# Where the operand sets of a transformer layer's last MLP third are made, and where a second set of buffers starts in memory

## The chip, the cores and the metric

The kernel runs on one core of one Trainium2 chip. The metric is the device time of one execution in microseconds (us); the time before is the median of three runs, 1019.47 us (1018.25, 1019.47 and 1020.26). Engines are named as in the profile: PE (TensorE), PEld (TensorE's weight load), DVE (VectorE), ACT (ScalarE), POOL (GpSimd), SP (SyncE, whose queue issues nearly all transfers).

## The reference

One decoder layer over 256 tokens of width 2048, in float32. Cut to what matters here:

```python
h = rms_norm(x, attn_norm_g)
proj = h @ w_in                       # q, k, v of 8 heads, and a pooled part
x = x + concat([attention(q, k, v), pooled(p)]) @ w_out

h = rms_norm(x, ffn_norm_g)           # the gated MLP; D_FF = 5632
u = h @ w_up                          # 2048 -> 2 * 5632
y = conv_b + sum(conv_w[i] * shifted(u, i) for i in range(3))
gate, val = split(y, 2)
x = x + (silu(gate) * val) @ w_down   # 5632 -> 2048
```

All matrix products keep float32 accuracy: each operand is split into a rounded high part and a low remainder, and three products (high by high, low by high, high by low) are summed.

## The kernel before

**Steps.** The whole kernel is a list of 362 steps. Each step uses one tile of weights of 128 x 1024 numbers. Two such tiles form a chunk of 1 MB, which SP loads into one of four `raw` buffers, in the order of use (`in_order`, line 131). Before a step, ACT makes the high part `wh` (`split_high`, line 163) and DVE the low part `wl` (`split_low`, line 167), five to six steps ahead of PE. DVE and ACT work strictly in the order in which the program emits their instructions, so what is emitted in a step's hooks (`after(u, f)`, line 622) stands in one line with the splits for the steps that follow. A chunk's `raw` buffer is released when its second tile has been split, and the release issues the next load (`release`, line 227).

**Stages.** Steps 0 to 97 hold the attention and the mixer, with a last block of 16 steps, the mixer's output projection by pairs. From step 98 the MLP runs in three thirds (`THIRDS`, line 57) of 8, 8 and 6 groups of 256 hidden columns. A third has an up projection of 8 steps for each group (64, 64, 48 steps), in which each group's gate and value pass through the convolution on DVE and ACT (`conv`, line 718: `L524` reads the value out of the PE's accumulators, then `L728`, `L735`, and later `L754`, `L761`), and then a down projection in two passes `b` = 0, 1 over output halves of 1024 columns, with one "quad" `j` of two steps for each group (16, 16, 12 steps a pass). In the text, "first third, up 14" is the step 14 after the first third's start. An up step and an ordinary half quad take 12 to 16 matmuls.

**Sums in place of products.** Some quads (`MIXED`, line 58) are done in the manner of Strassen and Winograd with 7 products in place of 8 (`quad_sums`, line 839: 12 matmuls of 512 columns in its first half, 9 in its second). Such a quad needs an operand set: sums and differences of the weights' quarters (`form_sums`, line 188), split in high and low, kept in a tile of 3072 numbers per partition. There are two such tiles. `s0` (index 0) belongs to a pool that lives through the whole MLP. `s1` (index 1) is opened anew for each down projection, behind a small tile `row`, in a pool whose memory the convolution's tiles `fs` and `y` use at other times (`open_temps`, line 634, with the down projection's opening at its step 2). Which quads use `s1` is set by `SECOND` (line 59) and `OUT_SECOND` (line 63): two of the mixer's, four in the first third, four in the second, two in the third, together 12. In the program before, `s0` starts 128 bytes past a multiple of 512 bytes in its partition, as all `wh` and `wl` buffers do when they are used in a down projection, and `s1` 64 bytes past one. In an operand set's quad, 9 of the 21 matmuls stream the set's columns through PE.

**Sets made early.** For most of these quads the set is made just before the quad. For two quads of each third it is made early, in the up projection, and parked in device memory (`STORED`, line 60). For such a quad, at an up step `at`:

- the chunk is loaded a first time as an extra chunk between two others (line 143), and for that time holds one of the four `raw` buffers;
- hook `at`: `early_sums` (line 193), on DVE one `L213` of 512 columns, one `L189` of 1024, one `L190` and one `L191` of 512, and one ACT copy;
- hook `at + 1`: `early_split` (line 198), one ACT copy and one `L213` of 1024 columns on DVE, and the release of the buffer;
- hook `at + 3`: `early_store` (line 202), two transfers from SP's queue to device memory, 0.5 MB of `t13` and 1.5 MB of `s0`, which serves as the scratch tile.

Later the quad's chunk is loaded in two halves, one of them from the stored `t13` (lines 136 and 137), and hook `u - ahead` loads the stored set of 1.5 MB (`load_set`, line 207, `L208`) into the quad's tile.

In the program before, each third makes its own two: the first and second third at up 22 and up 38, the third at up 22 and up 30. The third's two are for pass 0, quad 4 and pass 1, quad 2; both quads use `s1`. In the first quad of a down projection the second output accumulator takes over the bank that the last group's value was in, so its first matmul waits until `L524` of the last group has read that bank.

Of the kernel before, what the change touches and what calls it, by code (L numbers as in the profile page):

```python
# [25 lines left out]
F32 = mybir.dt.float32  # L26
# [5 lines left out]
P = 128  # L32
# [24 lines left out]
THIRDS = ((0, 8), (8, 16), (16, 22))  # L57
MIXED = {8: ((0, 3, 5, 6), (0, 3, 5, 6)), 6: ((0, 3, 4), (0, 2, 3))}
SECOND = {8: ((5,), (0, 3, 6)), 6: ((4,), (2,))}
STORED = {8: ((0, 5, 7), (1, 5, 6)), 6: ((0, 4, 5), (1, 2, 6))}  # L60
SUMMED = {n: sorted(set(a + b)) for n, (a, b) in MIXED.items()}
OUT_MIXED = (2, 3, 5, 6)
OUT_SECOND = (3, 6)
# [25 lines left out]
def layer(ctx: ExitStack, tc: tile.TileContext, xT, xtok, wts, par, rel_d, ident_d, icnt_d, out):  # L89
# [28 lines left out]
    raws, wparts, shift, late = {}, {}, {}, {}  # L118
    seven, stored, extra = {}, {}, {}
# [82 lines left out]
    def early_store(c):  # L202
        stored[c] = (dram.tile([P, HALF], F32, name=f"t{c}"), dram.tile([P, 3072], F32, name=f"s{c}"))
        nc.sync.dma_start(stored[c][0], late["t13"])
        nc.sync.dma_start(stored[c][1], late["tile"][0].bitcast(F32))

    def load_set(c, i):
        nc.sync.dma_start(late["tile"][i].bitcast(F32), stored[c][1])  # L208
# [370 lines left out]
    steps, hooks = [], []  # L579
# [29 lines left out]
    def feat_block(act, post, alloc=acc):  # L609
        box, runs = {}, []  # L610
        for i, k0 in enumerate(XK):
            def run(u, i=i, k0=k0):
                if i == 0:
                    box["ps"] = alloc("ps_feat")
                feat_half(u, act(), k0, box["ps"], i == 0, i == 3)
                if i == 3:
                    post(box["ps"])
            run.shift = SHIFT
            runs.append([run])
        return runs  # L620

    def after(u, f):

        hooks.append((u, f))

    def seven_tiles(pool, i):
        s = pool.tile([P, 3072], F32R, name=f"s{i}", tag=f"s{i}")
        late.setdefault("tile", {})[i] = s
        return [[s[:, :512], s[:, 512:1024]], [s[:, 1024:2048], s[:, 2048:]]]
# [4 lines left out]
    def open_temps(down):  # L634

        if "ctx" in late:
            late["ctx"].close()
        late["ctx"] = ExitStack()
        late["temps"] = late["ctx"].enter_context(tc.tile_pool(name="temps", bufs=1))
        if down:  # L640
            late["temps"].tile([P, 72], F32, name="row")
            late["s"][1] = seven_tiles(late["temps"], 1)

    def open_heads():
# [5 lines left out]
    def open_late():  # L650
        ectx.close()
        pool = ctx.enter_context(tc.tile_pool(name="late", bufs=1))
        late["pool"] = pool
        late["x2"] = pool.tile([P, NT, D], F32, name="x2")
        nc.sync.dma_start(late["x2"], xtok)
        sx = pool.tile([P, 4, 4, 2, P], F32R, name="sx")
        late["sx"] = [sx[:, i] for i in range(4)]
        late["s"] = [seven_tiles(pool, 0), None]
        open_temps(False)
        late["ss"] = pool.tile([P, NT, D // 512], F32, name="ss")  # L660
        late["t13"] = pool.tile([P, HALF], F32, name="t13")
# [80 lines left out]
    def gate(ps, g):  # L742
        def then(y):
            nc.scalar.activation(y, y, AF.Silu)
            late["gate"] = y
        conv(ps, 2 * g, 0, then)

    def value(ps, g, j):
        if j == 0:
            late["hid"] = keep.tile([P, KT, 2, S], F32R, name="hid", tag="c")  # L750
        hid, ks, mixed = late["hid"], slice(2 * j, 2 * j + 2), j in late["mixed"]

        def then(y):
            nc.vector.tensor_tensor(y, y, late["gate"], op=OP.mult)  # L754
            nc.scalar.activation(hid[:, ks, 0, :], y, AF.Copy)  # L755
            if mixed:
                token_sums(y)
            late["y"] = y

        def low():  # L760
            nc.vector.tensor_tensor(hid[:, ks, 1, :], late["y"], hid[:, ks, 0, :].bitcast(F32), op=OP.subtract)  # L761
            if mixed:
                sums_split(j, part=0)

        conv(ps, NF + 2 * g, 1, then)
        later(3, low)
        if mixed:
            later(4, lambda: sums_split(j, part=1))
# [272 lines left out]
    for b in range(2):  # L1041
# [3 lines left out]
        at = st["q", b, "end"] + (3 if b else 7)  # L1045
        if b == 0:
            after(at - 6, lambda: st.__setitem__(("q", 0), head_norm(st["qraw"], "qn", keep, "c")))
        for j in range(4):
            h, u = 4 * b + j, at + 2 * j
# [17 lines left out]
    for i, j in enumerate(OUT_MIXED):  # L1067
        after(o0 + 6 + 2 * i, lambda j=j: mixed_sums(OUT_ORDER[j]))
        after(o0 + 7 + 2 * i, lambda i=i: sums_split(i))
    after(len(steps) - 1, lambda: open_temps(True))  # L1070
    steps += down_pair(1, 8, False, "mixer")
    f0 = len(steps)
    after(f0 - 1, lambda: open_temps(False))
    after(f0 - 1, lambda: x2_T(1))
    after(f0 - 1, lambda: [square_sum(b, t) for t in range(NT) for b in (2, 3)])
# [2 lines left out]
    after(f0 + 3, lambda: x2_T(3))  # L1078
    after(f0 + 4, row2)

    for n, (g0, g1) in enumerate(THIRDS):
        nq, u0 = g1 - g0, len(steps)
        for i, (b, j, ahead) in enumerate(STORED[nq]):
            u = u0 + 8 * nq + b * 2 * nq + 2 * j
            at = u0 + 22 + 2 * nq * i - 4 * i * (nq < 8)
            extra[(at + 4) // 2] = u // 2
            after(at, early_sums)
            after(at + 1, early_split)
            after(at + 3, lambda c=u // 2: early_store(c))
            after(u - ahead, lambda c=u // 2, i=int(j in SECOND[nq][b]): load_set(c, i))  # L1090
        after(len(steps), lambda nq=g1 - g0: late.__setitem__("mixed", range(len(SUMMED[nq]))))
        for g in range(g0, g1):
            one = feat_block(lambda: late["h"], lambda ps, g=g: gate(ps, g),
                             acc if g > g0 else smalls if n else aux)
            two = feat_block(lambda: late["h"], lambda ps, g=g, j=g - g0: value(ps, g, j))
            steps += one + two if g else [step for both in zip(one, two) for step in both]
        after(len(steps) + 2, lambda: open_temps(True))
        for bp in range(2):
            steps += down_pair(bp, g1 - g0, n == len(THIRDS) - 1)
        after(len(steps) - 1, lambda n=n: open_temps(False) if n < len(THIRDS) - 1 else late["ctx"].close())  # L1100

    for u, f in hooks:
        steps[u].append(f)
    n = len(steps)
# [14 lines left out]
    for u in range(n):  # L1119
        ahead = u + AHEAD + 1  # L1120
# [97 lines left out]
```

## Time and profile before

| | us |
|---|---|
| three runs | 1018.25, 1019.47, 1020.26 |
| the profiled execution, its own time | 1018.5 |
| its span on the core | 1016.7 |
| PE busy in the span | 1007.4 |
| PEld / DVE / ACT / POOL busy | 863.0 / 855.8 / 589.0 / 102.4 |
| first third, up / down start at | 289.1 / 468.9 |
| second third, up / down start at | 551.0 / 728.5 |
| last third, up / down start at | 810.7 / 943.8 |

The profile's page gives sums over the span; the groups, waits, chain, windows and timeline are views of the same execution. In a window's row stand the window's length, the busy time of each engine in it with the number of instructions, the granted share of TensorE's clock ("PEclk"), the transfers' share and their rate. In a timeline row stand start, duration, engine, line, operation, tiles and, in brackets, the engine's idle time before it and what ended that. In the chain's rows stand start, duration, engine, what it writes, line and count.

### The profile page before, as it was taken

What the parts mean: (1) busy time and instruction counts of PE and PEld (TensorE: products, weight loads), DVE (VectorE), ACT (ScalarE), POOL (GpSimd) and SP (SyncE); (2) the same over time, 40 slices, a digit from 0 to 9 for tenths busy, and PEclk for the clock granted to TensorE, in tenths of its full rate; (3) what the DMA queues carried; (4) which work ended last, traced back from release to release, by engine and by line L of the source; (5) the groups of instructions that cost most, each with busy time, mean ns of one, the idle gap of its engine ahead of it and who ended that gap; (6) DMA issues with size and microseconds to landing.
All of it is one profiled execution on the core that took longest, in us unless ns stands there. A gap on an engine that the chain in (4) does not pass through costs nothing.

```text
span 1016.7 us, 13717 instructions
## 1 busy us (share of the span) xinstructions
PE 1007.4 (99%) x5229; PEld 863.0 (85%) x5229; DVE 855.8 (84%) x1105; ACT 589.0 (58%) x803; POOL 102.4 (10%) x110
## 2 busy tenths in 40 slices
PE   9999999999999999999999999999999999999998
PEld 8788888888888888888888888888888888888777
DVE  5998776888997888979985898898998579888975
ACT  6855665565665656656555565665556555556642
POOL 0220004600001111000000111100000002110010
PEclk9999999999999999999999999999999999999999
DMA  9785544474565575854887657676467774677494
GB/s 336 280 265 180 196 165 157 167 289 166 190 224 169 204 290 207 330 187 146 310 291 231 231 179 257 240 298 236 170 269 231 290 246 166 208 289 291 168 330 123
DMA packets 36801, 233.81 MB, mean 230 GB/s; under 512 B 4264, under 2 KB 5160, under 8 KB 12416
## 3 DMA queue, kind: packets, MB, share of 16 engines
q1 hardware_dynamic: 34000, 224.15, 60.7%
q0 software_dynamic: 2736, 8.78, 4.4%
q8 instruction: 41, 0.67, 0.3%
q14 instruction: 24, 0.20, 0.1%
HBM read 211.56 MB, written 15.07 MB: 223 GB/s over the span
## 4 chain that ended last, share of the span: by engine, by line
PE 90%; DVE 4%; DMA 3%; ACT 1%; issue 1%; SPq 0%; DVEq 0%; ACTq 0%
PE ps_feat L251 34%; PE ps_feat L253 17%; PE ps_down L866 15%; PE ps_tok L238 9%; PE ps_p L806 7%; PE ps_down L806 6%; DMA raw<-in_wts 2%; DVE wl L170 1%; DMA s<-s 1%; ACT wh L165 1%; PE ps_pool L260 1%; DVE y L735 1%; PE ps_s L468 1%; PE ps_down L888 0%; PE ps_T L455 0%
## 5 line engine op out<-in xcount | busy, mean ns | idle before, releaser
L170 DVE TENSOR_TENSOR wl<-raw,wh 128x1024 fp32r<-128x1024 f32 x358 | 440.9, 1246 | 72.6 <-ACT wh L165 29.5
L251 PE MATMUL ps_feat<-x2h,wh 128*128 128x512 f32 x1408 | 488.8, 392 | 0.0
L165 ACT ACTIVATE wh<-raw 128x1024 fp32r<-128x1024 f32 x358 | 368.1, 1050 | 112.6 <-DVE raw L189 69.6
L253 PE MATMUL ps_feat<-x2h,wl 128*128 128x256 f32 x1408 | 393.5, 280 | 0.0
L251 PEld LDWEIGHTS ps_feat<-x2h,wh 128*128 128x128 f32 x1408 | 264.3, 188 | 58.2
L253 PEld LDWEIGHTS ps_feat<-x2h,wl 128*128 128x128 f32 x1408 | 264.3, 188 | 0.1
L730 ACT ACTIVATE y<-fs,pv 128x256 f32<-128x256 f32 x88 | 48.2, 595 | 64.7 <-DVE fs L728 64.7
L866 PE MATMUL ps_down<-wh,hid 128*128 128x512 f32 x336 | 84.4, 394 | 0.0
L735 DVE SCALAR_TENSOR_TENSOR y<-fs,pv,y 128x255 f32<-128x255 f32 (+1 forms) x176 | 80.9, 481 | 3.2
L866 PEld LDWEIGHTS ps_down<-wh,hid 128*128 128x128 f32 x336 | 63.8, 190 | 13.7
L780 POOL TENSOR_TENSOR s<-y 128x128 f32<-128x128 f32 x24 | 32.4, 1352 | 348.9 <-DVE y L754 348.9
L211 ACT ACTIVATE s<-raw 128x512 fp32r<-128x512 f32 (+1 forms) x54 | 45.3, 839 | 15.3 <-DVE raw L191 15.3
L896 POOL DMA_DIRECT2D x<-st x13 | 11.6, 939 | 387.1 <-ACT st L971 315.2
L251 PE MATMUL ps_feat<-xh,wh 128*128 128x512 f32 x128 | 46.3, 402 | 0.0
L866 PE MATMUL ps_down<-wl,hid 128*128 128x512 f32 x168 | 45.3, 392 | 0.0
L520 ACT ACTIVATE fs<-ps_feat 128x512 f32<-128x512 f32 (+1 forms) x46 | 26.2, 570 | 22.2 <-PE ps_feat L253 22.2
L866 PEld LDWEIGHTS ps_down<-wl,hid 128*128 128x128 f32 x168 | 32.0, 190 | 6.8
L755 ACT ACTIVATE hid<-y 128x512 fp32r<-128x512 f32 x22 | 13.9, 633 | 38.6 <-DVE y L754 38.6
L253 PE MATMUL ps_feat<-xh,wl 128*128 128x256 f32 x128 | 35.8, 280 | 0.0
L238 PE MATMUL ps_tok<-wh,xh 128*128 128x512 f32 x128 | 35.5, 399 | 0.0
L245 PE MATMUL ps_v<-wh,xh 128*128 128x512 f32 x128 | 34.8, 394 | 0.0
L238 PE MATMUL ps_tok<-wh,cat 128*128 128x512 f32 x128 | 34.4, 390 | 0.0
(240 smaller groups left out, 1261.8 us busy)
## 6 DMA issues: line engine op xcount, KB each, us to landing
raw<-in_wts SPq DMA_DIRECT2D x177, 1024.0 KB, 5.1
s<-s SPq DMA_DIRECT2D x12, 1536.0 KB, 11.3
x<-st POOLq DMA_DIRECT2D x11, 512.0 KB, 8.0
raw<-in_wts SPq DMA_DIRECT2D x10, 512.0 KB, 6.7
t<-t SPq DMA_DIRECT2D x6, 512.0 KB, 8.9
raw<-t SPq DMA_DIRECT2D x6, 512.0 KB, 8.6
x<-in_xtok SPq DMA_DIRECT2D x1, 2048.0 KB, 9.1
raw<-in_wts SPq DMA_DIRECT2D x7, 256.0 KB, 5.5
```

What stands on the lines that cost most here:

```text
L165: nc.scalar.activation(wparts[u][0], raw(u - 1 if u - 1 in seven else u + 1 if u in seven else u), AF.Copy)
L170: nc.vector.tensor_tensor(wl, raw(u - 1 if u - 1 in seven else u + 1 if u in seven else u), wh.bitcast(F32), op=OP.subtract)
L211: nc.scalar.activation(parts[0], w, AF.Copy)
L238: nc.tensor.matmul(ps[:, t, :], act[:, k0 + k, a, t * P:(t + 1) * P], w[:, k * 512:(k + 1) * 512], start=(first and k == 0 and n == 0), st ...
L245: nc.tensor.matmul(ps[:, t, :], act[:, k, a, t * P:(t + 1) * P], w[i], start=(first and n == 0), stop=(last and n == 2))
L251: nc.tensor.matmul(ps, wh[:, ws], act[:, k, :, :], start=(first and n == 0), stop=False, skip_group_check=True)
L253: nc.tensor.matmul(ps[:, S:], wl[:, ws], act[:, k, 0, :], start=False, stop=(last and n == len(ks) - 1), skip_group_check=True)
L730: nc.scalar.activation(y[:, m, :], u[:, m, :], AF.Identity, scale=cw[m][2], bias=col(C_CB + f0_ + m))
L735: nc.vector.scalar_tensor_tensor(y[:, m, d:], u[:, m, :S - d], cw[m][2 - d], y[:, m, d:], op0=OP.mult, op1=OP.add)
L780: eng.tensor_tensor(s[:, n, :], a, b, op=op)
L806: nc.tensor.matmul(ps, act[a], w[i], start=(first and n == 0), stop=(last and n == 2), skip_group_check=skip)
L866: nc.tensor.matmul(bank(t, b), hid(order[j] + h, t)[a], part(w, b if h == 0 else 1 - b)[i], start=(n == 0 and h == 0 and (fresh or j == no ...
```

## The change

The table of sets made early now names the third `n` in which a set is made, the up step `at`, the third `m`, the pass `b` and the quad `j` that uses it, and how many steps ahead of the quad it is loaded back. The first third makes three sets, at up 14, 30 and 46, in place of two at 22 and 38; the third of them is the last third's first (pass 0, quad 4). The second third's two are as before. The last third makes only its second one (pass 1, quad 2), at up 22 in place of 30. Which quads use stored sets and when the sets are loaded back stays the same. The loop that sets the hooks moves behind the loop over the thirds, since it needs every third's first step.

The small tile ahead of `s1` grows from 72 to 88 numbers, 64 bytes, so that `s1` starts 128 bytes past a multiple of 512 bytes in place of 64.

```diff
-STORED = {8: ((0, 5, 7), (1, 5, 6)), 6: ((0, 4, 5), (1, 2, 6))}
+STORED = ((0, 14, 0, 0, 5, 7), (0, 30, 0, 1, 5, 6), (0, 46, 2, 0, 4, 5), (1, 22, 1, 0, 5, 7), (1, 38, 1, 1, 5, 6),
+          (2, 22, 2, 1, 2, 6))
...
         if down:
-            late["temps"].tile([P, 72], F32, name="row")
+            late["temps"].tile([P, 88], F32, name="row")
             late["s"][1] = seven_tiles(late["temps"], 1)
...
+    third = []
     for n, (g0, g1) in enumerate(THIRDS):
-        nq, u0 = g1 - g0, len(steps)
-        for i, (b, j, ahead) in enumerate(STORED[nq]):
-            u = u0 + 8 * nq + b * 2 * nq + 2 * j
-            at = u0 + 22 + 2 * nq * i - 4 * i * (nq < 8)
-            extra[(at + 4) // 2] = u // 2
-            after(at, early_sums)
-            after(at + 1, early_split)
-            after(at + 3, lambda c=u // 2: early_store(c))
-            after(u - ahead, lambda c=u // 2, i=int(j in SECOND[nq][b]): load_set(c, i))
+        nq = g1 - g0
+        third.append((len(steps), nq))
...
+    for n, at, m, b, j, ahead in STORED:
+        at += third[n][0]
+        u0, nq = third[m]
+        u = u0 + 8 * nq + b * 2 * nq + 2 * j
+        extra[(at + 4) // 2] = u // 2
+        after(at, early_sums)
+        after(at + 1, early_split)
+        after(at + 3, lambda c=u // 2: early_store(c))
+        after(u - ahead, lambda c=u // 2, i=int(j in SECOND[nq][b]): load_set(c, i))
```

## The prediction

> **What bounds the kernel now.** I read the page first, then the chain of waits, then the few places where PE idles, then the same places one third earlier.
>
> ```profile
> span 1016.7 us, 13717 instructions
> PE 1007.4 (99%) x5229; PEld 863.0 (85%) x5229; DVE 855.8 (84%) x1105; ACT 589.0 (58%) x803; POOL 102.4 (10%) x110
> ...
> PE 90%; DVE 4%; DMA 3%; ACT 1%; issue 1%; SPq 0%; DVEq 0%; ACTq 0%
> ```
>
> PE is busy nearly throughout, so a change can only win where PE idles, where its clock is reduced, or where a matmul is slower than its neighbours. The timeline of PE, and the waits of its weight load behind 900 us, show two idle places in the MLP, both in the last third's first down pass:
>
> ```profile
> PEld ps_down L806 <- DVE fs L524: 2.6, 1, 2.6
> ...
> 950.26 0.98 PE L806 MATMUL ps_down<-s,hid 128*128 128x512 f32 x3 [2.22 <-DVE fs L524]
> 967.69 0.84 PE L806 MATMUL ps_down<-s,hid 128*128 128x512 f32 x3
> 970.47 0.71 PE L806 MATMUL ps_p<-s,hid 128*128 128x512 f32 x2 [1.94 <-DMA s<-s]
> ```
>
> The windows give what follows them and, in the last two rows, the first three half quads of the down projection in the last and in the second third:
>
> ```profile
> 951.50:954.90 3.40, 3.40 (x9) 2.63 (x9) 3.29 (x7) 1.69 (x4) 0.00 (x0) 0.50 0.46 152
> 972.00:975.30 3.30, 3.30 (x9) 2.53 (x8) 3.23 (x4) 2.98 (x4) 0.00 (x0) 0.50 1.10 418
> 943.78:955.43 11.65, 9.43 (x36) 7.25 (x34) 10.67 (x16) 7.48 (x12) 0.00 (x0) 0.85 0.69 228
> 728.54:736.05 7.51, 7.51 (x35) 6.20 (x34) 6.95 (x11) 4.01 (x7) 0.00 (x0) 1.00 0.76 266
> ```
>
> The granted clock is 0.50 for about 3.4 us soon after each stall. The first stall with its slow stretch costs 11.65 - 7.51 = 4.14 us. The second: three matmuls from 967.69 at 0.227 us (2.04 / 9 in the chain's rows under part 2) end their turns at 968.37, PE goes on at 970.47, so 2.10 us, and half of a 3.4 us stretch, 1.7; together 3.8 us.
>
> **Why they are there.** The first stalled matmul needs a bank that `L524` must have read. DVE's rows of the second third (first two, then SP's) and of the last (two, then the chain's transfer), and PE's starts of the two down projections and of the second third's quad 4:
>
> ```profile
> 729.38 0.69 DVE L524 TENSOR_TENSOR fs<-ps_feat,fs 128x512 f32<-128x512 f32 x1 [0.28 <-ACT fs L520]
> 741.51 0.68 DVE L761 TENSOR_TENSOR hid<-y,hid 128x512 fp32r<-128x512 f32 x1
> 742.27 0.33 SPq L208 DMA_DIRECT2D s<-s  x1
> 949.52 0.69 DVE L524 TENSOR_TENSOR fs<-ps_feat,fs 128x512 f32<-128x512 f32 x1 [0.20 <-ACT fs L520]
> 961.64 0.68 DVE L761 TENSOR_TENSOR hid<-y,hid 128x512 fp32r<-128x512 f32 x1
> 962.41 7.92 DMA s<-s
> ...
> 728.54 0.63 PE L806 MATMUL ps_p<-s,hid 128*128 128x512 f32 x2
> 748.97 0.84 PE L866 MATMUL ps_down<-wh,hid 128*128 128x512 f32 x3
> 943.78 0.63 PE L806 MATMUL ps_p<-s,hid 128*128 128x512 f32 x2
> ```
>
> In the second third `L524` comes 0.84 us after the down projection's start; PE needs it 18 matmuls in, at 728.54 + 18 x 0.227 = 732.63, and it ends at 730.07: 2.6 us to spare. In the last third it comes 949.52 - 943.78 = 5.74 us after, 4.90 late. `L761` is the last to use the memory that `s1` takes, so the load of the stored set waits for it. From `L524` to that load is 12.89 us in both thirds (742.27 - 729.38, 962.41 - 949.52). So both stalls hang on one lag of DVE.
>
> **Part 1, the sets.** A set's instructions on DVE:
>
> ```profile
> 901.26 0.69 DVE L213 TENSOR_TENSOR s<-raw,s 128x512 fp32r<-128x512 f32 x1 [1.09 <-ACT s L211]
> 901.87 1.22 DVE L189 TENSOR_TENSOR t<-raw 128x1024 f32<-128x1024 f32 x1
> 903.12 0.69 DVE L190 TENSOR_TENSOR raw<-raw,t 128x512 f32<-128x512 f32 x1
> 903.85 0.69 DVE L191 TENSOR_TENSOR raw<-raw 128x512 f32<-128x512 f32 x1
> 905.67 1.23 DVE L213 TENSOR_TENSOR s<-raw,s 128x1024 fp32r<-128x1024 f32 x1
> ```
>
> That is 4.52 us. The last third pays two, 9.0 us, within 8 steps, and DVE has 18 steps left. Windows of 8 up steps, three of the first third (up 38 to 62) and one of the last (up 30 to 38):
>
> ```profile
> 396.81:419.00 22.19, 22.19 (x131) 19.54 (x129) 20.78 (x28) 13.53 (x18) 0.00 (x0) 1.00 0.71 254
> 419.00:441.18 22.18, 22.18 (x130) 19.53 (x129) 19.39 (x27) 14.35 (x19) 0.00 (x0) 1.00 0.81 309
> 441.18:463.37 22.19, 22.19 (x130) 19.54 (x129) 18.69 (x24) 11.77 (x15) 0.00 (x0) 1.00 0.45 149
> 893.86:916.04 22.18, 22.18 (x130) 19.52 (x129) 20.77 (x27) 12.27 (x17) 2.75 (x3) 1.00 0.74 266
> ```
>
> *Taken from the last third:* one set of 4.52 us, and the other moves 8 steps earlier. What remains, one set at up 22, is what the second third has, which has a second at 38 and still starts its down projection with DVE waiting for ACT (0.28 us idle before `L524`). The lag that remains is 0. The first stall goes: gain 4.14 us.
>
> *The second stall* does not go with it. Without lag the set's load is issued 0.84 + 12.89 us after 943.78, at 957.51. PE wants it where the second third's quad 4 starts, 748.97 - 728.54 = 20.43 us in, at 964.21. The landing times:
>
> ```profile
> DMA to landing us min/median/max: 7.9/9.0/10.4
> DMA to landing us min/median/max: 9.0/9.0/9.0
> ```
>
> The first row is over all six loads of sets, the second the one at 742.27. With 7.92 us it lands at 965.43, and PE goes on 0.14 us later (970.33 to 970.47 before): 1.36 us of stall; with 9.0 us it is 2.4. I take 1.6, nearer to this load's own 7.92, since the loads ahead of it stay the same. What is late next is the clock. Idle PE of 2.1 us was followed by a halved clock; the shortest idle of which I know the sequel is in the heads:
>
> ```profile
> 50.48 0.73 PE L866 MATMUL ps_down<-wh,xh 128*128 128x512 f32 x2 [0.78 <-ACT v L431]
> 50.70:54.10 3.40, 3.40 (x16) 2.79 (x16) 3.40 (x5) 3.40 (x5) 3.23 (x4) 1.00 1.04 378
> ```
>
> There 0.8 us left the clock at 1.00. A stall of 1.6 lies between, so I charge half of 1.7 us, 0.85. The second stall then costs 1.6 + 0.85 = 2.45 in place of 3.8: gain 1.35 us (bounds: 3.8 if the load is in time, -0.3 with 2.4 and a full 1.7). The Trainium skill, "TensorE: Matmul & The Clock Gate", Part 1, has the clock halve only after about one whole idle window of some 3.4 us; the slow stretch of 3.4 us agrees with its window, the 2.1 us that sufficed here do not. By that rule the remaining stall would be free of the slow stretch, and the sum larger by 0.85 us.
>
> *Given to the first third:* one more set, and all three at other steps: 4.52 us on DVE, two ACT copies, one extra load of 1 MB, stores of 0.5 and 1.5 MB through SP. DVE's idle time in the three windows is 1.41 + 2.79 + 3.50 = 7.7 us, and the set now at 38, which falls in the first of them, moves to 30. So DVE is even again before up 64. PE's row is full (22.19 of 22.19) where a set was made before, so the `wl` made ahead cover one set; SP's store waits for DVE, with the next chunks' loads behind it, as at 22 and 38 already. Its 3 MB add 136 GB/s to a window of 22 us; beside the 149 of the third that is less than the 309 that the second has. Cost 0; without that cover 4.5 us, and 1.7 more if the clock drops. The second third's sets, the loads back and the half chunks are not moved.
>
> **Part 2, 64 bytes.** In the chain, a quad with `s0` (first pair), one with `s1` (second) and the `s0` quad behind it:
>
> ```profile
> 484.77 2.72 PE ps_p L806 x12
> 487.49 2.04 PE ps_down L806 x9
> ...
> 494.97 2.78 PE ps_p L806 x12
> 497.75 2.08 PE ps_down L806 x9
> 499.82 2.74 PE ps_p L806 x12
> 502.57 2.04 PE ps_down L806 x9
> ```
>
> 4.76, 4.86 and 4.78 us: `s1` costs 0.10 and 0.02 behind it. If the start address is the cause, the new one is `s0`'s, and 12 quads give 12 x 0.12 = 1.44 us; if it is something else, such as the place in memory, 0. A loss is excluded as far as the offset decides, for `s0` has the new one. I take 1.44, because what else differs between the tiles touches DVE and SP, not PE's reading.
>
> **Sum.** 4.14 + 1.35 + 1.44 = 6.9 us. Against the profiled execution's own 1018.5 that is 1011.6; it lies 1.0 under the median of the runs, within their spread. The mean of the four known times is 1019.1, and I forecast 1019.1 - 6.9 = **1012.2**.
>
> **Rivals.**
>
> *The load is in time* (10%): both stalls go, 4.14 + 3.8 + 1.44 = 9.4, 1009.7 us. For it: with fewer transfers in the last third the landing may shorten. Against: it would need 6.6 us, and the shortest of six is 7.9.
>
> *The second stall stays whole* (15%): landing as in the second third, 9.0, and a halved clock: 4.14 - 0.3 + 1.44 = 5.3, 1013.8 us.
>
> *The offset does nothing* (15%): 4.14 + 1.35 = 5.5, 1013.6 us. For it: `s1` also lies elsewhere in the partition. The Trainium skill, "SBUF — State Buffer", Specifications, gives lines of 16 bytes; 64 and 128 are both multiples, so by that page the offset would be free and this rival right, but the 0.10 us are in the trace.
>
> *The lag has another cause* (4%): the last third, shorter by 16 steps, starts its down projection late whatever is made early; then part 2 alone, 1017.7 us. Against it: nothing else in its up projection differs from the second third's.
>
> *Slower: the debt moves to the first third* (3%). Three sets are 13.6 us. If all but 2.6 us of them is unpaid at up 64, `L524` is 11 us late there, PE loses 11 - 2.6 = 8.4 and 1.7 by the clock, 10.1 against the 6.9 won: 1022.3 us. It decides from a debt of 2.6 + 6.9 - 1.7 = 7.8 us. Against it: two sets in 8 steps left only 4.9 in the last third, and here they are 16 steps apart.
>
> The forecast has 53%. What a measurement can tell from no change is about 0.2%, 2 us. Faster by more: 53 + 10 + 15 + 15 = 93%; within: 4%; slower: 3%. The range goes from the full gain on the fastest run, 1018.25 - 9.4 = 1008.9, to the first stall alone with part of a set uncovered: 1018.5 - 4.1 + 2 = 1016.4.
>
> **What would show it.** Right: no PE wait on `L524` behind 900 us; `L524` under 1 us after the last down projection's start; one wait on the set's transfer of 1.4 to 2.4 us some 20 us later; all 12 `s1` quads at 4.76; PE full in the first third's up. Wrong: PE idle in the first third, `s1` quads at 4.86, or the transfer's wait gone.

## The result, and the profile after

The changed kernel takes 1009.87 us, the median of four runs (1009.83 to 1010.19), against 1019.12 for four runs of the kernel before (1018.25 to 1020.26). The ratio is 0.9909, with a 95% interval of 0.9892 to 0.9926: faster by 0.9%. The profiled execution took 1010.19 us with a span of 1008.4, 8.3 us less than before. First the page's head and chain, then PE's timeline where the last third's first down pass wanted the set:

```profile
span 1008.4 us, 13717 instructions
PE 1002.6 (99%) x5229; PEld 860.7 (85%) x5229; DVE 855.1 (85%) x1105; ACT 588.1 (58%) x803; POOL 103.4 (10%) x110
...
PE 94%; DVE 2%; DMA 1%; ACT 1%; issue 1%; SPq 0%; DVEq 0%; ACTq 0%
...
961.87 0.84 PE L807 MATMUL ps_down<-s,hid 128*128 128x512 f32 x3
963.96 0.70 PE L807 MATMUL ps_p<-s,hid 128*128 128x512 f32 x2 [1.25 <-DMA s<-s]
```

Lines from 61 on stand one lower than before, so `L525` is the old `L524`, `L762` the old `L761`. The wait on `L525` is gone. The wait on the set's transfer is left, shorter: three matmuls from 961.87 at 0.227 us end their turns at 962.55, and PE goes on at 963.96, 1.41 us later (2.10 before). The chain that led to the first wait, DVE's timeline first, then PE's start of the down projection, then the transfer from the chain:

```profile
942.96 0.69 DVE L525 TENSOR_TENSOR fs<-ps_feat,fs 128x512 f32<-128x512 f32 x1 [0.22 <-ACT fs L521]
955.07 0.69 DVE L762 TENSOR_TENSOR hid<-y,hid 128x512 fp32r<-128x512 f32 x1
...
942.12 0.63 PE L807 MATMUL ps_p<-s,hid 128*128 128x512 f32 x2
...
955.84 7.98 DMA s<-s
```

`L525` comes 0.84 us after the start of the down projection, as in the second third before; the load is issued 13.72 us after it (forecast: 0.84 + 12.89 = 13.73) and takes 7.98 us.

The windows show where the 8.3 us went. The first three rows are of the kernel after: the last third from its down projection's start to the start of pass 1, the stretch behind the remaining wait, and the stretch from the first quad of sums, in the heads, to the last down projection. The last two are of the kernel before, for the first and the third of these:

```profile
942.12:974.26 32.14, 30.89 (x137) 25.27 (x136) 30.15 (x34) 17.08 (x22) 2.70 (x3) 1.00 0.72 266
964.00:967.40 3.40, 3.40 (x15) 2.83 (x16) 3.29 (x5) 3.01 (x4) 0.00 (x0) 1.00 0.99 383
66.47:942.12 875.65, 875.65 (x4671) 755.87 (x4669) 749.16 (x964) 512.48 (x702) 85.55 (x80) 1.00 0.64 227
...
943.78:982.42 38.64, 34.49 (x137) 27.44 (x136) 34.42 (x40) 21.24 (x27) 2.70 (x3) 0.91 0.73 260
66.95:943.78 876.83, 876.83 (x4671) 755.80 (x4670) 745.52 (x958) 509.12 (x697) 84.77 (x79) 1.00 0.64 226
```

The first down pass of the last third is 38.64 - 32.14 = 6.50 us shorter, and the clock behind the wait stays at 1.00. The long stretch, in which PE is busy throughout in both kernels, is 1.18 us shorter; it holds 10 of the 12 quads that use `s1`. The last such quad, in pass 1, is taken at the same 0.12. The other 0.48 us lie before 67 us, in the heads, which the change does not touch. The quads, from the chain after:

```profile
494.24 2.72 PE ps_p L807 x12
496.96 2.04 PE ps_down L807 x9
499.00 2.72 PE ps_p L807 x12
501.72 2.04 PE ps_down L807 x9
```

The first pair is the `s1` quad of 4.86 us before, now 4.76, and the `s0` quad behind it has lost its 0.02. Ten of the 12 `s1` quads take 4.76 us and one 4.78; the one behind the remaining wait takes 5.03.

The first third now makes three sets. Windows of 8 of its up steps from up 14, 30 and 46, each with DVE's work for one set in it (from 334.93, 380.65 and 423.43), and then DVE's `L525` of the third's last group:

```profile
329.53:351.72 22.19, 22.19 (x131) 19.54 (x130) 19.37 (x26) 12.05 (x17) 3.90 (x4) 1.00 0.69 245
373.90:396.09 22.19, 22.19 (x131) 19.54 (x129) 20.54 (x27) 11.63 (x16) 3.40 (x3) 1.00 0.64 220
418.27:440.46 22.19, 22.19 (x130) 19.54 (x129) 20.79 (x27) 13.59 (x18) 0.00 (x0) 1.00 0.69 247
...
469.03 0.69 DVE L525 TENSOR_TENSOR fs<-ps_feat,fs 128x512 f32<-128x512 f32 x1 [0.28 <-ACT fs L521]
```

PE is full in all three, and DVE has 2.82, 1.65 and 1.40 us of idle time in them. The first third's down projection starts at 468.19, so `L525` comes 0.84 us after it there too, with DVE waiting for ACT: nothing of the third set is left unpaid.

### The profile page after: what moved, and what is told of

It reads as the page before. It is cut to its first block, busy times and chain, and to the rows that moved or that the text cites. A ratio compares the mean times of both kernels' runs of the same rounds, so it can differ in the third digit from the quotient of the medians.

```text
span 1008.4 us, 13717 instructions
## 1 busy us (share of the span) xinstructions
PE 1002.6 (99%) x5229; PEld 860.7 (85%) x5229; DVE 855.1 (85%) x1105; ACT 588.1 (58%) x803; POOL 103.4 (10%) x110
## 4 chain that ended last, share of the span: by engine, by line
PE 94%; DVE 2%; DMA 1%; ACT 1%; issue 1%; SPq 0%; DVEq 0%; ACTq 0%
PE ps_feat L252 35%; PE ps_feat L254 18%; PE ps_down L867 15%; PE ps_tok L239 9%; PE ps_p L807 7%; PE ps_down L807 5%; PE ps_v L246 2%; DMA s<-s 1%; DVE wl L171 1%; DMA raw<-in_wts 1%; PE ps_pool L261 1%; PE ps_s L469 1%; PE ps_down L889 0%; ACT wh L166 0%; DVE y L736 0%
```

## The experiments

**The changed kernel again**, for comparison on one chip with the sets alone, the offset alone and the first runs of the early load.

> The changed kernel as it stands, for comparison on the same chip. Expected 1009.9 us, 9 us under the kernel before, with one wait on the set's transfer of 1.2 to 1.4 us in the last third's first down pass. By the rival that the clock decides by chance, some executions would show a halved clock of 3.4 us behind that wait, and the runs would spread by up to 1.7 us.

1009.72 us (1009.24 to 1010.76), the kernel before 1018.39 beside it, ratio 0.9918 (0.9904 to 0.9931). One wait on the transfer, no halved clock behind it. Over the whole of an execution the granted clock was 1.000 in all four, where it was 0.998 in the run below with one slow stretch (the remaining set at up 30).

**The sets alone.**

```diff
-            late["temps"].tile([P, 88], F32, name="row")
+            late["temps"].tile([P, 72], F32, name="row")
```

> Part 1 alone: the sets are made where the change has them, and the second operand set's buffers stay 64 bytes past a multiple of 512. If the two parts are independent and the offset is worth 12 quads of 0.12 us, the time is 1.4 us over the changed kernel: 1011.3 us, with quads of 4.86 us where the second set's buffers are read. If the offset's gain came from something else, it is the changed kernel's 1009.9 us.

1011.05 us (1010.63 to 1011.58), ratio to the kernel before 0.9930 (0.9917 to 0.9942); 1.3 us over the changed kernel. The quads, from its chain:

```profile
493.62 2.78 PE ps_p L807 x12
496.40 2.08 PE ps_down L807 x9
498.48 2.74 PE ps_p L807 x12
501.22 2.04 PE ps_down L807 x9
```

The 4.86 and 4.78 us are back, the wait on the transfer is there (1.39 us), no other. The two parts add up.

**The offset alone**: the kernel before with 88 in place of 72.

> Part 2 alone: the kernel before with the second operand set's buffers 128 bytes past a multiple of 512. If the offset works by itself: 1.4 us under the kernel before, 12 quads at 4.76 us, and both stalls in the last third stay (waits of about 2.2 us on L524 and 1.9 us on the set's transfer, the clock at 0.50 for 3.4 us behind each). If the stalls depend on the offset in any way, they change too, and the gain is over 2 us.

1017.35 us (1016.11 to 1018.81), ratio 0.9990 (0.9981 to 0.9999): 1.0 us by the medians. The quads take 4.76 us, but for the one behind the second wait (7.61), and the long stretch from the first quad of sums to the last down projection takes 875.62 us, 1.21 less than before. Both stalls stay, but not with the sizes expected. PE's timeline, and the windows behind the two stalls:

```profile
947.73 0.98 PE L806 MATMUL ps_down<-s,hid 128*128 128x512 f32 x3 [2.24 <-DVE fs L524]
968.93 1.62 PE L806 MATMUL ps_p<-s,hid 128*128 128x512 f32 x3 [4.55 <-DVE raw L191]
...
947.70:951.10 3.40, 3.37 (x15) 2.76 (x16) 3.32 (x6) 2.04 (x3) 0.00 (x0) 1.00 0.58 202
968.90:972.30 3.40, 3.37 (x8) 2.75 (x9) 2.25 (x2) 2.01 (x2) 0.00 (x0) 0.50 1.05 417
```

(The second wait ends with the set's transfer, which landed at 968.80; the DVE instruction named there was long done.) Here the first idle time, no shorter than in the kernel before, was not followed by a halved clock, and the second stall grew to 4.7 us. Counted from the start of the down projection, PE came to the quad 1.6 us sooner than in the kernel before, and the transfer, with 8.9 us from issue to landing in place of 7.9, let it go on 1.0 us later. So the two stalls are not two prices to add: the landing of the set ends them both, and what PE loses before it is taken off the wait.

**DVE's work alone**, put back into the changed kernel. (This run and the next three have one execution each, on another chip, where the kernel before took 1018.44 us.)

```diff
+    def dve_like(sizes):
+        for n in sizes:
+            w = late["t13"][:, :n]
+            nc.vector.tensor_tensor(w, w, w, op=OP.subtract)
+    after(third[2][0] + 30, lambda: dve_like((512, 1024, 512, 512)))
+    after(third[2][0] + 31, lambda: dve_like((1024,)))
```

> The changed kernel with five more DVE instructions in the last third, four at up 30 and one at up 31, of a set's sizes (512, 1024, 512, 512, 1024 columns), on a tile that nobody reads; no transfer, no ACT copy and no raw buffer is added. If the lag of DVE alone makes the stalls, L524 of the last group is about 4.9 us late again, PE waits about 2.3 us on it and then on the set's transfer, and the time rises by 5 to 7 us to about 1016. If the second set's transfers or its raw buffer made them, nothing changes: 1009.8 us and one wait of 1.4 us.

1016.81 us in its one execution, 7.1 over the changed kernel. PE's timeline, and the window behind the second wait:

```profile
948.24 0.98 PE L807 MATMUL ps_down<-s,hid 128*128 128x512 f32 x3 [1.04 <-DVE fs L525]
968.94 1.00 PE L807 MATMUL ps_p<-s,hid 128*128 128x512 f32 x3 [4.04 <-DMA s<-s]
...
969.70:973.00 3.30, 3.30 (x9) 2.59 (x8) 2.36 (x3) 2.55 (x3) 0.00 (x0) 0.50 1.10 431
```

Both waits are back with no transfer added, the first shorter and the second longer than in the kernel before, and the clock halves behind the second. The lag of `L525` is 3.7 us rather than 4.9. A set's two ACT copies are not in this run; that they make the difference is likely but not shown.

**The transfers alone**: in the kernel before, the last third's second set is loaded and stored but not computed.

```diff
+            if n == 2 and i == 1:
+                after(at + 1, lambda: release("extra"))
+            else:
                 after(at, early_sums)
                 after(at + 1, early_split)
```

> The kernel before with the last third's second early set not made: its extra chunk is loaded and released and both stores go out, but DVE's and ACT's instructions for it are left out, so the set that pass 1, quad 2 reads is not its own. If DVE's lag makes the stalls: no wait on L524, one wait of 1.4 us on the transfer, and the time is that of the sets-only kernel, about 1011 us. If the transfers make them: both stalls stay, about 1018.5 us.

1010.80 us, that of the sets alone. No wait on `L524`, one of 1.31 us where the set's transfer is wanted, the clock at 1.00. With the run before it this settles the cause: the work of a second set on DVE (with its ACT copies) makes the lag, its transfers do not.

**The remaining set 8 steps later.**

```diff
-          (2, 22, 2, 1, 2, 6))
+          (2, 30, 2, 1, 2, 6))
```

> The changed kernel with the last third's remaining set at up 30 in place of up 22. If DVE repays about 3.5 to 4.7 us in 8 steps once the hidden sums of the third's first four groups are done, some 1 us is open when the down projection starts: L524 is 1.1 us late, which its 2.6 us to spare cover, and the set's load comes 1.1 us later, so that the one wait is 2.5 us and the time 1.1 us over the changed kernel, 2.8 us where the clock halves behind it. If the debt is repaid by then, nothing changes.

1013.90 us, 4 us over the changed kernel and more than was expected. `L525` comes 944.72 - 942.33 = 2.39 us after the down projection's start, 1.55 late, which PE did not notice; the load comes as much later, and the window behind its wait has the halved clock:

```profile
966.06 1.62 PE L807 MATMUL ps_p<-s,hid 128*128 128x512 f32 x3 [3.15 <-DMA s<-s]
...
966.10:969.40 3.30, 3.30 (x8) 2.63 (x9) 2.77 (x3) 2.14 (x3) 0.00 (x0) 0.50 1.02 401
```

So one set at up 30 is already too late; moving the first set away is only part of the gain, and the step from 30 to 22 gives some 4 us of it.

**The first third's sets 8 steps later.**

```diff
-STORED = ((0, 14, 0, 0, 5, 7), (0, 30, 0, 1, 5, 6), (0, 46, 2, 0, 4, 5), ...
+STORED = ((0, 22, 0, 0, 5, 7), (0, 38, 0, 1, 5, 6), (0, 54, 2, 0, 4, 5), ...
```

> The changed kernel with the first third's three sets at up 22, 38 and 54 in place of 14, 30 and 46. By the theory that a lag of up to 2 us is covered there (2.6 us to spare at L524, some 4 us at the first third's stored set), L524 comes some 2 us late in the first third, PE waits for nothing there and the time is the changed kernel's. By the rival that the debt moves to the first third, PE waits on L524 or on the set's transfer there, and the time rises by 1 us or more.

1019.98 us: my theory fell, and the rival got its stall, from something that neither had. The waits between 440 and 482 us, and PE's timeline:

```profile
DVE s L214 <- ACT s L212: 8.4, 2, 7.3
ACT s L212 <- DMA s<-s: 7.9, 1, 7.9
PEld ps_down L807 <- DVE fs L525: 6.2, 1, 6.2
...
479.62 1.65 PE L807 MATMUL ps_down<-s,hid 128*128 128x512 f32 x3 [5.80 <-DVE fs L525]
...
478.00:484.60 6.60, 4.98 (x12) 3.92 (x13) 6.26 (x10) 3.41 (x6) 0.00 (x0) 0.50 0.78 259
```

(The last row is a window.) The early set is formed in `s0`, and the store of 1.5 MB, issued at 451.26 and landed 13.7 us later, still reads `s0` when ACT wants to form the first quad's own set in it. ACT waits 7.9 us for that transfer, DVE for ACT, `L525` behind them for its turn, and PE for `L525`. From the first third's down projection to the second's is 737.18 - 468.44 = 268.74 us, against 727.34 - 468.19 = 259.15 in the changed kernel: 9.6 us lost.

**The load of the set sooner**, against the wait that is left.

```diff
-... (0, 46, 2, 0, 4, 5)
+... (0, 46, 2, 0, 4, 7)
...
-        later(3, low)
+        later(2 if g in LASTS else 3, low)      # LASTS: the last group of each third
...
-        after(len(steps) + 2, lambda: open_temps(True))
+        after(len(steps) + 1, lambda: open_temps(True))
```

> The changed kernel with the last group's low part of the hidden values (L761) one step earlier in DVE's order, the pool of the second operand set opened one step sooner and the last third's first set loaded two steps sooner. If the remaining stall of 1.4 us hangs on L761, the load is issued some 6 to 7 us sooner, lands before PE wants it, the wait goes and the time is 1.4 us under the changed kernel: 1008.5 us. If the transfers set it (the load behind a chunk's load, at 7.9 us or more to landing), the wait stays at 1 us or more and the time is the same. If DVE's wait for ACT in the middle of its line costs more than it wins, it is slower.

1009.06 us (1008.01 to 1010.15). The wait is gone. (Lines stand two lower than in the kernel before: `L763` is the old `L761`.) DVE's and SP's timeline, the landing time of that load, and the window that answers to 942.12 to 974.26 above:

```profile
950.26 0.69 DVE L763 TENSOR_TENSOR hid<-y,hid 128x512 fp32r<-128x512 f32 x1 [0.76 <-ACT hid L757]
951.04 0.33 SPq L210 DMA_DIRECT2D s<-s  x1
DMA to landing us min/median/max: 6.5/6.5/6.5
...
943.56:974.19 30.63, 30.63 (x138) 25.34 (x136) 29.15 (x34) 17.09 (x22) 1.71 (x3) 1.00 0.74 267
```

The load is issued 7.5 us after the down projection's start in place of 13.7, PE is full, and the stretch takes 30.63 us in place of 32.14. DVE's 0.76 us of waiting for ACT cost PE nothing. The runs of the two kernels spread by 1.5 and 2.1 us, so both were timed again.

> The changed kernel once more, beside the kernel with the early load, for a closer comparison on one chip: about 1009.8 us, one wait of 1.4 us in the last third's first down pass, no halved clock behind it.

> The kernel with the early load once more. Its trace has lost the wait of 1.4 us and is 1.6 us shorter from the first quad of sums on. If that is its worth, the median is 1.4 to 1.6 us under the changed kernel beside it; if the runs differ by what happens before that quad, the two medians lie within 1 us and their runs overlap.

1010.22 us (1009.31 to 1010.60) and 1008.50 us (1007.57 to 1009.18); ratios to the kernel before 0.9915 (0.9902 to 0.9929) and 0.9899 (0.9886 to 0.9913). Over both timings the changed kernel's nine runs have a mean of 1009.98, the eight with the early load 1008.75: 1.2 us, with an interval of about 0.7 to either side. It is the fastest kernel of this study.

**Other starts of the second operand set**: the small tile with 104 and with 56 numbers, so that `s1` starts at 192 and at 0.

> The changed kernel with a small tile of 104 numbers, so that the second operand set's buffers start 192 bytes past a multiple of 512. If starts that are multiples of 128 are what TensorE streams at full speed, its 12 quads take 4.86 us here; if only starts below 128 are slow, 4.76 us.

> The changed kernel with a small tile of 56 numbers, so that the second operand set's buffers start at a multiple of 512. If starts that are multiples of 128 are fast: 4.76 us for each of its 12 quads; if only starts from 128 on are fast: 4.86 us.

One execution each, 1011.86 us with 192 and 1010.71 with 0. The same `s1` quad in the chains of the two, 192 first:

```profile
494.25 2.79 PE ps_p L807 x12
497.04 2.09 PE ps_down L807 x9
```

```profile
493.58 2.77 PE ps_p L807 x12
496.35 2.08 PE ps_down L807 x9
```

4.88 and 4.85 us. Both rules fell: neither multiples of 128 nor all starts from 128 on are fast. Of 0, 64, 128 and 192 only 128 is, the start (past a multiple of 512) of the `wh` and `wl` tiles that such a quad streams beside the set. Whether it has to be that number or the same one for all operands of a quad was not tried, and stays open.

## Why the prediction was right, and where it was not

**The first stall** (4.14 us): right in cause and place. The lag is DVE's, as the two runs that parted DVE's work from the transfers show, and `L525` is back at 0.84 us.

**The second stall** (gain forecast 1.35): right that it stays, with the issue of the load within 0.01 us; its size was 1.41 us where I took 1.6. The step that failed is the charge for the clock behind it, "so I charge half of 1.7 us, 0.85": the clock stayed at 1.00 in all seven executions profiled with a wait of this size. The last section shows why: no idle time as short as this one was followed by half the clock, wherever it fell. Without that charge and with 1.41 us, the gain is 3.8 - 1.41 = 2.4, and with the first stall's 4.14 it is 6.5, against 6.50 - 0.12 (the one `s1` quad in it, taken at what the others gain) = 6.4 measured.

**The two stalls as two terms.** Their sum was right, but not because each has its price. The run with the offset alone shows that the landing of the set ends both. PE goes on with that quad 970.47 - 943.78 = 26.69 us after the down projection's start before and 963.96 - 942.12 = 21.84 after: 4.85 us, nearly the lag of 4.90. The other 1.65 of the 6.50 lie behind that point, where the clock was halved before; the `s1` quad's gain is in them. These are the real terms. By this account, ending the first stall without moving the landing would have gained nothing.

**The first third** (cost 0): right; PE is full where its sets are made. The reasons given were DVE's idle time, the `wl` made ahead and the transfers' rate. That the store must have left `s0` before the down projection forms its own set there was not among them, and it is what stopped the third set at up 54: up 46 is early enough (the store is issued at 431.1, and ACT forms the first quad's set from 454.40 without a wait), up 54 costs 9.6 us. So the slower rival exists, 8 steps away, with another mechanism than the debt for which I priced it.

**The offset** (1.44): 10 quads gave 1.18 us; with 0.12 for each of the two in the last third, 1.42 together. Of those two, the one behind the wait cannot be read by itself. The rival that it does nothing fell. The Trainium skill, "SBUF — State Buffer", Specifications, has lines of 16 bytes, and all four starts tried are multiples of 16: the lines give no reason for the quads to differ. They do differ, and the measurement decides.

**The sum.** 6.9 forecast; 6.38 + 1.42 = 7.8 us of the span's 8.3 are the change's, and 0.48 are chance in the heads. The time, 2.3 us under the forecast, is in the range, near the rival of both stalls gone, though that one is refuted: the wait is still there. The missing 0.85 us and the chance account for some 1.3 of it; the rest lies between the profiled executions and the medians, whose spread of 2 us before does not resolve it.

## What to carry to other kernels

An engine that works in order pays its debts at the next place where something waits for it; look for the stage with idle time on that engine, and place the work so far ahead that the debt is repaid, with its scratch memory free again, before that place. Where two waits follow from one lag, take the landing of the later one as the price. And when one tile of several like ones is streamed a little slower, compare where they start.

## What the runs showed of the hardware that was not expected

**The clock.** From the rows above, PE's idle time was followed by a granted clock of 0.50 where it was 1.94, 2.22, 3.15, 4.04 and 4.55 us, and of 1.00 where it was 1.25 and, in the offset's run, 2.24. The heads of the run with the early load add one more, PE's timeline first and then the window behind the idle time:

```profile
51.45 0.73 PE L868 MATMUL ps_down<-wh,xh 128*128 128x512 f32 x2 [1.54 <-ACT v L433]
...
51.40:54.80 3.40, 3.35 (x15) 2.78 (x16) 3.40 (x5) 3.40 (x5) 3.40 (x5) 1.00 1.04 376
```

So about 2 us of idle time went both ways. What decided it is where the idle time lay. Each slow stretch is 3.41 us long, or twice that, and within one execution the slow stretches start whole multiples of 3.413 us apart: in the kernel before, 971.97 - 951.49 = 20.48 = 6 x 3.413. These are windows of that grid, first four of the kernel before, then four of the offset's run. There the slow stretch starts at 967.61, and the grid is counted back from it (967.61 - 6 x 3.413 = 947.13):

```profile
948.08:951.49 3.41, 1.23 (x5) 1.03 (x6) 3.16 (x4) 1.93 (x4) 0.00 (x0) 1.00 0.89 279
951.49:954.90 3.41, 3.41 (x9) 2.65 (x9) 3.31 (x7) 1.70 (x4) 0.00 (x0) 0.50 0.46 151
968.56:971.97 3.41, 1.50 (x7) 1.27 (x8) 3.31 (x5) 1.60 (x2) 0.00 (x0) 1.00 0.91 332
971.97:975.38 3.41, 3.41 (x10) 2.63 (x9) 3.34 (x4) 3.01 (x4) 0.00 (x0) 0.50 1.09 414
...
943.71:947.13 3.42, 1.78 (x8) 1.13 (x6) 2.65 (x4) 3.01 (x4) 0.00 (x0) 1.00 0.39 86
947.13:950.54 3.41, 2.81 (x12) 2.31 (x13) 3.34 (x6) 2.04 (x3) 0.00 (x0) 1.00 0.61 257
964.19:967.61 3.42, 0.19 (x1) 0.00 (x0) 3.35 (x5) 0.16 (x1) 0.00 (x0) 1.00 0.97 400
967.61:974.43 6.82, 5.50 (x13) 4.42 (x14) 4.73 (x6) 3.96 (x5) 0.00 (x0) 0.50 1.00 375
```

The idle time in a window is its length less PE's busy time, the second and third number of its row. The windows ahead of the slow stretches have 2.18, 1.91 and 3.23 us of it. The idle time of 2.24 us in the offset's run lay across a border of the grid, 1.64 us in one window and 0.60 in the next, and the clock stayed at 1.00. In all 14 profiled executions, behind their first 10 us, every window at full clock with 1.91 us or more of idle PE was followed by half the clock, and none with 1.64 or less was; between the two nothing was measured. So in these runs idle time of up to 1.64 us was free of the slow stretch, and some 2 us cost 1.7 us more or nothing, by the place in the grid.

By the Trainium skill, "TensorE: Matmul & The Clock Gate", Part 1, it takes one idle window of some 3.4 us, and the window runs free of the kernel. The length and the grid agree with these traces; that the whole window has to be idle does not, since 1.91 us sufficed.

**The start address.** A set that starts 0, 64 or 192 bytes past a multiple of 512 costs 0.09, 0.10 and 0.12 us more in a quad of 21 matmuls than one at 128, and 0.02 to 0.05 in the quad behind it, which reads none of it.

**The first 67 us.** They differed by 2.4 us between executions (the heads' first quad of sums begins at 65.5 us in one and at 67.9 in another) with the same work there; differences of about 1 us between kernels are better read from a window behind them than from the times.
